# Raw first products of each later layer, corrected for the norm afterwards

## The chip, the cores and the metric

One core of one Trainium2 chip runs the whole program. The metric is the device time of one execution in microseconds (us). Engines are named as the profile does: PE (TensorE), DVE (VectorE), ACT (ScalarE), POOL (GpSimd), SP (the queue that issues the DMAs).

## What is computed

A model of three blocks over 512 positions of width 1024, all in float32: a first block (swiglu, a mixer, a second swiglu, then "ple", a gated product with a second input p, and a norm), and two layers of a second block. The parts around the change, cut from the reference:

```python
gate = jax.nn.sigmoid(rmsnorm(h, norm_ple[i]) @ w_ple_gate[i])
h = h + gate * (p[i] @ w_ple[i])
...
x = rmsnorm(h, norm_final)
for l in range(DEPTH_2):
    mod = c_act @ w_ada[l] + b_ada[l]
    shift, scale, gate = jnp.split(mod, 3, axis=-1)
    h = rms_norm(x, norm_g[l]) * (1.0 + scale[:, None, :]) + shift[:, None, :]
    u = h @ w_in[l]
    rg_x, rg_z, ml_x, ml_o, ml_z = jnp.split(u, split_pts, axis=-1)
    ...
    y = jnp.concatenate([y_rg, y_ml], axis=-1) @ w_out[l]
    x = x + gate[:, None, :] * y
```

A norm divides each position by the root of its mean square, so it is known only when all 1024 features of the position are there.

## The kernel before, in words

Activations lie with 128 features on the partitions and the 512 positions along a row; a width of 1024 is eight such tiles h(0) to h(7). A float32 product is made of three matmuls of 128x512 (`mm3`, L125 to L127): the input is split into a high and a low part (xnh by ACT, xnl by DVE), the weights into whi and wlo, and hi*hi, lo*hi and hi*lo are summed in PSUM. One such product of a 128x128 block takes three matmuls 0.227 us apart.

Weights come as one stream (`Stream`, L56): chunks of eight blocks, 512 KB, loaded by DMAs of the SP queue, split by ACT (whi, L96) and DVE (wlo, L98), two chunks ahead of their use. `hold` and `release` set these splits back at the end of ple and of out0.

A norm (`Norm`, L130) squares each tile as it is finished (ACT, L149), adds the squares on DVE (L155) and POOL (L153), lets PE sum the columns (L165), takes the root in ten small DVE steps (L206 to L213), spreads it over the partitions by four PE transposes (L195) and copies it to `nrow` (ACT, L198).

ple makes eight tiles h(m): the gate product, DVE multiplies it with nrow (L1282), ACT takes tanh (L1283), and two DVE steps (L1287, L1288) finish h. `between` (L1345 on) then makes two norms in one, and `modulate` makes the input of layer 0: per tile a multiply mt (DVE L1330 or POOL L1328), ACT xnh (L1337), DVE mx (L1338) and DVE xnl (L1341). Only then start the products. The first four of a layer (ml_x, outputs 16 to 19, here called raw products where they don't wait for the norm) give `cpad`, the input of a convolution on DVE (L1507, L1509), whose result, split as xch and xcl, feeds the next step, "qkv0". The order of the products behind is a written string `LAYER` (P24 and so on). At the end of each layer `out` makes the next x from 16 products a tile; in layer 0 `renorm` follows, which is the same chain once more (seam 1). While layer 0 runs, the normalised x is written to memory tile by tile and read back for the residual in out.

A list of small steps (`Fill`) that prepares the layers (the modulation from c, gates, constants) is run beside the swiglu of ffn2, with a rate R2; it also loads and splits p (pp0h, pp0l and so on).

Of the kernel before, what the change touches and what calls it, by code (L numbers as in the profile page):

```python
# [38 lines left out]
R1, R2 = 0.27, 0.26  # L39
# [8 lines left out]
GAPS = {"base": 288, "ffn1": 320, "ffn2": 0, "lay": 320, "mix2": 224, "ple": 256}  # L48
# [81 lines left out]
class Norm:  # L130
# [3 lines left out]
    def __init__(self, k, n, pool=None, tail=False):  # L134
        self.k, self.n, self.i = k, n, 0
        self.tail, self.head = tail, None
        self.pool = pool or k.work
        self.acc = []

    def add(self, src, scale=1.0):  # L140


        k, i = self.k, self.i
        own = i < 2 or (self.tail and i == self.n - 1)
        if own:
            sq = self.pool.tile([128, T], F32, name="nacc", bufs=3 if self.pool is k.work else 6)
# [3 lines left out]
        if own:  # L150
            self.acc.append(sq)
        elif i % 2:
            k.nc.gpsimd.tensor_add(self.acc[1], self.acc[1], sq)  # L153
        else:
            k.nc.vector.tensor_add(self.acc[0], self.acc[0], sq)  # L155
        self.i += 1
        if self.i == self.n - self.tail:
            eng = k.nc.vector if self.tail else k.nc.gpsimd
            eng.tensor_add(self.acc[0], self.acc[0], self.acc[1])
# [1016 lines left out]
def second_prepare(k, pool, ins):  # L1176
# [15 lines left out]
    for l in range(2):  # L1192
# [8 lines left out]
        L.bif = k.const2.tile([128, 8], F32, name=f"bif{l}")  # L1201
        L.v = lambda name, l=l: k.vec[:, VEC[f"{name}.{l}"][0]:VEC[f"{name}.{l}"][0] + VEC[f"{name}.{l}"][1]]
# [13 lines left out]
        def acc(i, L=L, boxes=boxes):  # L1216
# [3 lines left out]
                                   op0=OP.mult, op1=OP.add, accum_out=L.mod[:, i:i + 1])  # L1220

# [54 lines left out]
def ple(k, pool, xs, norm, pt, on_tile, early):  # L1276
# [3 lines left out]
    def gate1(m, pg):  # L1280
        ts[m] = pool.tile([128, T], F32, name="pleg", bufs=2)
# [16 lines left out]
    for m in range(8):  # L1298
# [12 lines left out]
        k.ws.hold = m == 7  # L1311
# [4 lines left out]
    early()  # L1316


def modulate(k, l, norm, gg, scr):
# [3 lines left out]
    xs, ts = [], []  # L1323
    with k.tc.tile_pool(name=f"modulate{l}", bufs=3) as tmp:
        def scale(d):
            t = tmp.tile([128, T], F32, name="mt", bufs=4)
# [4 lines left out]
            ts.append(t)  # L1331
        for d in range(3):
            scale(d)
        for d in range(8):
            x = tmp.tile([128, T], F32, name="mx")
            hi, lo = xtile(k, "xnh"), xtile(k, "xnl")
            nc.scalar.activation(hi, ts[d], AF.Identity, scale=gg[:, d:d + 1], bias=L.mod[:, d:d + 1])  # L1337
            v.tensor_scalar(x, ts[d], gg[:, d:d + 1], L.mod[:, d:d + 1], op0=OP.mult, op1=OP.add)  # L1338
            if d + 3 < 8:
                scale(d + 3)  # L1340
            v.tensor_sub(lo, x, hi.bitcast(F32))  # L1341
            xs.append((hi, lo))
            if d == 1:
                k.ws.release()
            k.dbg(f"hh{l}{d}", x)  # L1345
    return xs


def between(k, scr, nf, ng):
# [3 lines left out]
    nc, v = k.nc, k.nc.vector  # L1353
    gg = k.work.tile([128, 8], F32, name="gg")
    gf = k.vec[:, VEC["norm_final"][0]:VEC["norm_final"][0] + 8]
    v.tensor_mul(gg, gf, k.lay[0].gs)
    nf.part1(root=False)
    ng.mean()
    ms = k.work.tile([128, 4], F32, name="nmt", bufs=2)
    v.scalar_tensor_tensor(ms, nf.ms, 1e-6, ng.ms, op0=OP.mult, op1=OP.add)  # L1360
    ng.col = k.work.tile([128, 4], F32, name="ncol", bufs=2)
    rsqrt(k, ng.col, ms)
    ng.part2()
    xs = modulate(k, 0, ng, gg, scr)
    rsqrt(k, nf.col, nf.ms)

    def root():
        nf.part2()

    def residual(d):  # L1370
        v.scalar_tensor_tensor(k.h[d], k.h[d], gf[:, d:d + 1], nf.row, op0=OP.mult, op1=OP.mult)
        nc.sync.dma_start(scr["x"][d], k.h[d])
        k.dbg(f"x2{d}", k.h[d])
    return xs, [root] + [lambda d=d: residual(d) for d in range(8)]


def renorm(k, l, norm, scr):
    norm.part1()
    norm.part2()
    xs = modulate(k, l, norm, k.lay[l].gs, scr)  # L1380
    return xs, [lambda d=d: k.nc.sync.dma_start(scr["x"][d], k.h[d]) for d in range(8)]
# [85 lines left out]
def layer(k, l, xs, aside, ins, scr, norm, out):  # L1467
# [4 lines left out]
    with ExitStack() as st:  # L1472
        pool = st.enter_context(k.tc.tile_pool(name=f"lay{l}", bufs=1))
        room(pool, "lay")
# [750 lines left out]
```

## Time and profile before

| | |
|---|---|
| median of 3 runs | 1997.68 us (1996.73 to 1998.62) |
| profiled execution, its own time | 1996.86 us |
| its span in the trace | 1995.1 us |
| busy: PE, DVE, ACT, POOL | 1931.2, 1311.4, 821.4, 164.4 us |
| mean granted PE clock | 0.982 |

The span is what the trace covers; the rest of the time lies around it. Stages of the span: ffn2 690 to 1061, ple 1061 to 1119, seam 0 to 1137, layer 0 to 1555 (out0 from 1466), seam 1 to 1571, layer 1 with its ending to 1995. A busy share is an average: what a step is worth is read from the wait that it ends.

### The profile page before, as it was taken

The page shows a single profiled execution, that of the slowest core. Times are in us where ns is not written, and L with a number is a line of the kernel's source. Part 1 is how long each engine was busy: PE and PEld are TensorE (multiplying, and loading weights), DVE is VectorE, ACT ScalarE, POOL GpSimd, SP SyncE. Part 2 cuts the span into 40 slices and gives each one's busy share as a digit, 9 for nine tenths or more (in the row PEclk, how much of TensorE's full clock was granted, in tenths as well). Part 3 has the DMA queues.
Part 4 walks back from the last instruction along what each step waited for, and adds up shares of the span by engine and source line. Part 5 has one row for each costly group of instructions (what it writes and reads, how often), then busy time and mean ns, then how long its engine had stood idle before and what let it go on. Part 6 is the DMA issues. An engine that isn't in the chain of part 4 may idle for free. (4 is left out here: it accounts for less than half of the span.)

```text
span 1995.1 us, 24709 instructions
## 1 busy us (share of the span) xinstructions
PE 1931.2 (97%) x9320; PEld 1581.3 (79%) x9320; DVE 1311.4 (66%) x2157; ACT 821.4 (41%) x1233; POOL 164.4 (8%) x225
## 2 busy tenths in 40 slices
PE   8999999998999999999999799999999899999997
PEld 6888888887867888888878687888888677887886
DVE  7766576678655575665666675887763666877843
ACT  5323232436555432232244445555432354555521
POOL 1000000111233100000001100101000100101001
PEclk9999999998899999999999899999999899999999
DMA  5335445465301365455433143222242243222241
GB/s 184 103 116 154 158 139 159 143 194 171 103 1 33 117 218 180 158 197 190 162 104 92 55 147 118 74 75 86 88 153 87 64 156 109 70 89 86 74 155 56
DMA packets 101400, 240.10 MB, mean 120 GB/s; under 512 B 24472, under 2 KB 37528, under 8 KB 101280
## 3 DMA queue, kind: packets, MB, share of 16 engines
q1 hardware_dynamic: 100592, 237.82, 37.6%
q8 instruction: 73, 1.20, 0.2%
q10 hardware_dynamic: 688, 0.70, 0.1%
q14 instruction: 47, 0.39, 0.1%
HBM read 216.19 MB, written 21.10 MB: 119 GB/s over the span
## 5 line engine op out<-in xcount | busy, mean ns | idle before, releaser
L98 DVE TENSOR_TENSOR wlo<-wstage,whi 128x1024 fp32r<-128x1024 f32 (+1 forms) x305 | 377.3, 1245 | 147.6 <-ACT whi L96 143.8
L96 ACT ACTIVATE whi<-wstage 128x1024 fp32r<-128x1024 f32 (+1 forms) x306 | 314.0, 1045 | 139.9 <-PE pasecond L126 43.1
L276 ACT ACTIVATE t<-t 128x512 f32<-128x512 f32 x44 | 27.9, 634 | 158.5 <-DVE t L275 158.5
L127 PE MATMUL pahead<-xnh,wlo 128*128 128x512 f32 x208 | 81.3, 391 | 3.4 <-DVE wlo L98 3.4
L125 PE MATMUL pahead<-xnh,whi 128*128 128x512 f32 x208 | 83.3, 400 | 0.0
L153 POOL TENSOR_TENSOR nacc<-nacc,nsq 128x512 f32<-128x512 f32 x20 | 26.8, 1343 | 680.9 <-ACT nsq L149 680.9
L126 PE MATMUL pahead<-xnl,whi 128*128 128x512 f32 x208 | 81.1, 390 | 0.0
L125 PE MATMUL pbfirst<-xnh,whi 128*128 128x512 f32 x176 | 70.4, 400 | 7.6 <-ACT whi L96 6.5
L125 PE MATMUL pbhead<-xnh,whi 128*128 128x512 f32 x192 | 76.9, 400 | 0.0
L1509 DVE SCALAR_TENSOR_TENSOR conv<-cpad,vec,conv 128x512 f32<-128x512 f32 x96 | 72.2, 752 | 5.6
L127 PE MATMUL pbhead<-xnh,wlo 128*128 128x512 f32 x192 | 75.5, 393 | 0.0
L126 PE MATMUL pbhead<-xnl,whi 128*128 128x512 f32 x192 | 75.3, 392 | 0.0
L126 PE MATMUL pbfirst<-xnl,whi 128*128 128x512 f32 x176 | 69.5, 395 | 0.3 <-DVE xnl L222 0.3
L127 PE MATMUL pbfirst<-xnh,wlo 128*128 128x512 f32 x176 | 69.2, 393 | 0.0
L125 PE MATMUL pbsecond<-xnh,whi 128*128 128x512 f32 x176 | 68.9, 392 | 0.0
L125 PE MATMUL pafirst<-xnh,whi 128*128 128x512 f32 x176 | 68.7, 390 | 0.0
L127 PE MATMUL pafirst<-xnh,wlo 128*128 128x512 f32 x176 | 68.6, 390 | 0.0
L127 PE MATMUL pbsecond<-xnh,wlo 128*128 128x512 f32 x176 | 68.5, 389 | 0.0
L126 PE MATMUL pbsecond<-xnl,whi 128*128 128x512 f32 x176 | 68.5, 389 | 0.0
L126 PE MATMUL pafirst<-xnl,whi 128*128 128x512 f32 x176 | 68.5, 389 | 0.0
L127 PE MATMUL pasecond<-xnh,wlo 128*128 128x512 f32 x176 | 68.5, 389 | 0.0
L125 PE MATMUL pasecond<-xnh,whi 128*128 128x512 f32 x176 | 68.5, 389 | 0.0
(762 smaller groups left out, 5229.9 us busy)
## 6 DMA issues: line engine op xcount, KB each, us to landing
wstage<-in_wpack_dram SPq DMA_DIRECT2D x304, 512.0 KB, 3.7
adaw<-in_wada_dram SPq DMA_DIRECT2D x48, 512.0 KB, 4.5
scr_v<-vv SPq DMA_DIRECT2D x16, 256.0 KB, 2.2
vr<-scr_v SPq DMA_DIRECT2D x16, 256.0 KB, 4.4
xr<-scr_x SPq DMA_DIRECT2D x16, 256.0 KB, 5.8
h<-in_xT_dram SPq DMA_DIRECT2D x8, 256.0 KB, 5.8
s5vw<-scr_wq SPq DMA_DIRECT2D x64, 32.0 KB, 2.0
s5vb<-in_s5bq_dram SPq DMA_DIRECT2D x8, 256.0 KB, 2.7
```

Of the source, the lines that this page charges most:

```text
L96: k.nc.scalar.activation(hi[:, s], st[:, s], AF.Copy)
L98: eng.tensor_sub(lo[:, s], st[:, s], hi[:, s].bitcast(F32))
L125: mm(ps, w[0], x[0], start=start, stop=False)
L126: mm(ps, w[0], x[1], start=False, stop=False)
L127: mm(ps, w[1], x[0], start=False, stop=stop)
L153: k.nc.gpsimd.tensor_add(self.acc[1], self.acc[1], sq)
L276: nc.scalar.activation(t1, t1, AF.Silu)
L1509: v.scalar_tensor_tensor(c, xp[:, 1 + j:1 + j + T], w(j), c, op0=OP.mult, op1=OP.add)
```

## The change

- Raw products. Position by position, norm and shift can be applied after the product: (h g r + s) W = r (h g) W + s W. So h(m) times its gain is split as it is made (`split_raw`: ACT xnh, DVE xnl; in ple and in out0), and the four ml_x products run on it in the order RAW. `raw_pad` then multiplies with nrow (DVE) and adds s W (ACT). s W comes from new steps in the fill of ffn2: 16 transposes, 4 copies, 8 loads of 512 KB and 8 sums on DVE.
- Norm steps at other products. The sums, the root and the transposes hang as hooks at products 8, 10 and 14 of RAW in layer 0 and 1, 3 and 9 in layer 1; a tile of the proper input, for the products from P24 on, at every second product after. It takes two DVE steps and one of ACT; POOL has no part in it.
- p is loaded and split at the start of ple, in a pool that both layers share, and no longer in the fill.
- In ple h(m) is written to memory raw, and out0 makes the norm of the residual with four transposes and eight DVE steps.
- The adds of tile 6's squares in ple stand behind tile 7; hold and release are gone; R2 is 0.30, two gaps between pools are larger.

```diff
+def split_raw(k, src, g, hi, lo):
+    k.nc.scalar.activation(hi, src, AF.Copy, scale=g)
+    k.nc.vector.scalar_tensor_tensor(lo, src, g, hi.bitcast(F32), op0=OP.mult, op1=OP.subtract)
+    return hi, lo
...
 def modulate(k, l, norm, gg):
-            if d % 2:
-                nc.gpsimd.tensor_mul(t, k.h[d], norm.row)
-            else:
-                v.tensor_mul(t, k.h[d], norm.wide)
...
-            nc.scalar.activation(hi, ts[d], AF.Identity, scale=gg[:, d:d + 1], bias=L.mod[:, d:d + 1])
-            v.tensor_scalar(x, ts[d], gg[:, d:d + 1], L.mod[:, d:d + 1], op0=OP.mult, op1=OP.add)
-            v.tensor_sub(lo, x, hi.bitcast(F32))
...
+        v.scalar_tensor_tensor(t, k.h[d], g, norm.wide if d == 0 else norm.row, op0=OP.mult, op1=OP.mult)
+        nc.scalar.activation(hi, t, AF.Identity, bias=b)
+        v.scalar_tensor_tensor(lo, t, b, hi.bitcast(F32), op0=OP.add, op1=OP.subtract)
...
+RAW = [(m, d) for m in range(4) for d in range(7)]
+RAW = RAW[:14] + [(0, 7)] + RAW[14:21] + [(1, 7)] + RAW[21:] + [(2, 7), (3, 7)]
+def seam(k, l, norm, gg, early, mean, at):
+    xs, tile = modulate(k, l, norm, gg)
+    hooks = dict(zip(at, (early, mean, norm.part2)))
+    for d in range(8):
+        hooks[at[2] + 1 + 2 * d] = lambda d=d: tile(d)
+    return xs, hooks
...
 def layer(k, l, raw, xs, hooks, aside, before, ins, scr, norm, out):
+        def raw_pad(i, ps):
...
+            v.tensor_mul(xp[:, 4:], ps, before.row)
+            nc.scalar.activation(xp[:, 4:], xp[:, 4:], AF.Identity, bias=L.sw[:, i:i + 1])
...
-        for m, ps in enumerate(proj4([16, 17, 18, 19])):
-            ml_pad(m, ps)
+        for n, (i, d) in enumerate(RAW):
+            mm3(k, banks[i], k.ws.get((win, d, 16 + i)), raw[d], d == 0, d == 7)
+            if n in hooks:
+                hooks[n]()
+            if d == 7:
+                raw_pad(i, banks[i])
...
+                nc.tensor.transpose(pb[:, j * 128:(j + 1) * 128], k.closing[:, j:j + 1].to_broadcast([128, 128]), k.ident)
+            if l == 0:
+                v.scalar_tensor_tensor(xr[m], xr[m], k.v("norm_final", m), pb, op0=OP.mult, op1=OP.mult)
...
+            if l == 0:
+                raw.append(split_raw(k, k.h[m], k.lay[1].gs[:, m:m + 1], xtile(k, "xnh"), tile("xnl", F32R)))
+                nc.sync.dma_start(scr["x"][1, m], k.h[m])
...
+        def done(m):
+            if m == 6:
+                raw.append(split_raw(k, k.h[m], gg[:, m:m + 1], k.ytile("xnh", F32R), k.ytile("xnl", F32R)))
+            nf.add(k.h[m], 1.0, later if m == 6 else None)
+            ng.add(k.h[m], k.v("norm_final", m), later if m == 6 else None)
+            for f in later if m == 7 else ():
+                f()
+            if m != 6:
+                raw.append(split_raw(k, k.h[m], gg[:, m:m + 1], k.ytile("xnh", F32R), k.ytile("xnl", F32R)))
+            nc.sync.dma_start(scr["x"][0, m], k.h[m])
...
+        for i in (1, 2, 3):
+            step(1.4, sacc, i)
```

The first place is ACT at the end of ffn2: gh is the split of a swiglu tile, t its gate, p the second input of ple. Before:

```order
431 L233 ACTIVATE gh<-t_8344 128x512
432 L96 ACTIVATE whi<-wstage 128x1024 x2
433 L233 ACTIVATE pp0h<-p_8415 128x512
434 L233 ACTIVATE pp1h<-p_8417 128x512
435 L276 ACTIVATE t_8427<-t_8427 128x512
436 L233 ACTIVATE gh<-t_8428 128x512
437 L221 ACTIVATE xnh<-h,vec 128x512
```

Now:

```order
438 L96 ACTIVATE whi<-wstage 128x1024
439 L283 ACT_TABLE_LOAD
440 L283 ACTIVATE t_8473<-t_8473 128x512
441 L240 ACTIVATE gh<-t_8474 128x512
442 L228 ACTIVATE xnh<-h,vec 128x512
```

The copies pp0h and pp1h are gone from here; they stand 20 rows on, at the start of ple, and a table load has come up to the last tile.

The second place is DVE in ple, one tile after another (h is its result, pleg its gate). Before:

```order
1087 L1282 TENSOR_TENSOR pleg<-pbple,nrow 128x512
1088 L98 TENSOR_TENSOR wlo<-wstage,whi 128x1024
1089 L1287 SCALAR_TENSOR_TENSOR pleg<-pleg,paple 128x512
1090 L1288 SCALAR_TENSOR_TENSOR h<-pleg,h 128x512
1091 L1282 TENSOR_TENSOR pleg<-pbple,nrow 128x512
```

Now:

```order
1117 L1319 TENSOR_TENSOR pleg<-pbple,nrow 128x512
1118 L98 TENSOR_TENSOR wlo<-wstage,whi 128x1024
1119 L1324 SCALAR_TENSOR_TENSOR pleg<-pleg,paple 128x512
1120 L1325 SCALAR_TENSOR_TENSOR h<-pleg,h 128x512
1121 L1357 SCALAR_TENSOR_TENSOR xnl<-h,gg,xnh 128x512
1122 L1319 TENSOR_TENSOR pleg<-pbple,nrow 128x512
```

The raw xnl, which needs ACT's xnh of the same tile, stands between h and the gate multiply of the next tile.

The third place is DVE behind the root of the norm in seam 0. Before:

```order
1115 L213 SCALAR_TENSOR_TENSOR ncol<-rsa,rsy 128x4
1116 L1330 TENSOR_TENSOR mt<-h,pm 128x512 x2
1117 L1338 TENSOR_SCALAR mx<-mt,gg,mod_5923 128x512
1118 L1341 TENSOR_TENSOR xnl<-mx,xnh 128x512
1119 L1338 TENSOR_SCALAR mx<-mt,gg,mod_5923 128x512
1120 L1330 TENSOR_TENSOR mt<-h,pm 128x512
1121 L1341 TENSOR_TENSOR xnl<-mx,xnh 128x512
```

Now:

```order
1150 L98 TENSOR_TENSOR wlo<-wstage,whi 128x1024
1151 L1529 TENSOR_TENSOR cpad<-pagates_9195,nrow 128x512
1152 L1370 SCALAR_TENSOR_TENSOR mt<-h,gg,pm 128x512
1153 L1373 SCALAR_TENSOR_TENSOR xnl<-mt,mod_5924,xnh 128x512
1154 L1370 SCALAR_TENSOR_TENSOR mt<-h,gg,nrow 128x512
1155 L1373 SCALAR_TENSOR_TENSOR xnl<-mt,mod_5924,xnh 128x512
```

Each xnl now follows its own mt directly, with ACT's xnh between them, and the multiplies that make cpad lie among the tiles.

## Rows read from the trace of the kernel before

**Rows 1.** The page, busy time of each engine (us, share of the span, instructions).

```profile
PE 1931.2 (97%) x9320; PEld 1581.3 (79%) x9320; DVE 1311.4 (66%) x2157; ACT 821.4 (41%) x1233; POOL 164.4 (8%) x225
```

**Rows 2.** Timeline of PE, ple, seam 0, qkv0 (start, duration, what; wait and releaser in brackets).

```profile
1061.33 0.39 PE L125 MATMUL paple<-xnh,whi 128*128 128x512 f32 x1
...
1118.17 0.39 PE L127 MATMUL pbple<-pp1h,wlo 128*128 128x512 f32 x1
...
1131.10 0.66 PE L195 MATMUL pm<-ident,ncol 128*128 128x128 f32 x2 [2.52 <-DVE ncol L213]
...
1134.45 0.79 PE L125 MATMUL pagates<-xnh,whi 128*128 128x512 f32 x1 [2.26 <-ACT xnh L1337]
...
1179.00 0.39 PE L126 MATMUL pbgates<-xcl,whi 128*128 128x512 f32 x1
```

**Rows 3.** Timeline of PE, end of out0 and qkv0 of layer 1.

```profile
1554.36 0.39 PE L127 MATMUL pbout<-ymh,wlo 128*128 128x512 f32 x1
...
1606.97 0.39 PE L126 MATMUL pbgates<-xcl,whi 128*128 128x512 f32 x1
```

**Rows 4.** Windows, seam 0 (span; busy PE, PEld, DVE, ACT, POOL; clock, DMA share, GB/s).

```profile
1124.00:1140.00 16.00, 8.91 (x29) 7.27 (x30) 9.67 (x26) 7.37 (x10) 3.79 (x3) 0.50 0.00 0
```

**Rows 5.** Timeline of PE, last tile of ffn2.

```profile
1036.21 0.49 PE L125 MATMUL pasecond<-gh,whi 128*128 128x512 f32 x1 [2.33 <-ACT gh L233]
```

**Rows 6.** Timeline of ACT, the split of p near the end of ffn2.

```profile
1030.18 0.63 ACT L233 ACTIVATE pp0h<-p 128x512 fp32r<-128x512 f32 x1 [4.53 <-DMA p<-in_pT_dram]
```

**Rows 7.** One line of PE, transposes (minimum/median/maximum ns, first and last start).

```profile
L1022 PE MATMUL pc<-ident,csm x8: 272/272/273, 555.3 to 556.0; 128*128 128x128 f32 x8
```

**Rows 8.** One line of DVE, the sums of the modulation in ffn2, same columns.

```profile
L1219 DVE CUSTOM_DVE_ANT_0 adaj<-adaw,b2c,vec x48: 1274/1278/1282, 710.2 to 1013.7; 128x1024 f32<-128x1024 f32 x48
```

**Rows 9.** Timeline of DVE, end of ffn2 and ple.

```profile
1053.06 0.68 DVE L305 SCALAR_TENSOR_TENSOR h<-pasecond,h 128x512 f32<-128x512 f32 x1
1054.53 0.75 DVE L222 SCALAR_TENSOR_TENSOR xnl<-h,vec,xnh 128x512 fp32r<-128x512 f32 x1 [0.80 <-ACT xnh L221]
1055.20 0.69 DVE L155 TENSOR_TENSOR nacc<-nacc,nsq 128x512 f32<-128x512 f32 x1
...
1075.97 1.23 DVE L98 TENSOR_TENSOR wlo<-wstage,whi 128x1024 fp32r<-128x1024 f32 x1 [1.65 <-ACT whi L96]
1077.12 0.68 DVE L1287 SCALAR_TENSOR_TENSOR pleg<-pleg,paple 128x512 f32<-128x512 f32 x1
1077.83 0.69 DVE L1288 SCALAR_TENSOR_TENSOR h<-pleg,h 128x512 f32<-128x512 f32 x1
...
1114.96 1.65 DVE L98 TENSOR_TENSOR wlo<-wstage,whi 128x1024 fp32r<-128x1024 f32 x1 [2.25 <-ACT whi L96]
...
1123.61 0.69 DVE L1288 SCALAR_TENSOR_TENSOR h<-pleg,h 128x512 f32<-128x512 f32 x1
```

**Rows 10.** Timeline of ACT, a tile of ple, and nrow of seam 0.

```profile
1112.20 0.63 ACT L149 ACTIVATE nsq<-h 128x512 f32<-128x512 f32 x1 [2.67 <-DVE h L1288]
1112.74 0.71 ACT L149 ACTIVATE nsq<-h,vec 128x512 f32<-128x512 f32 x1
1113.36 0.61 ACT L1283 ACTIVATE pleg<-pleg 128x512 f32<-128x512 f32 x1
1113.88 1.05 ACT L96 ACTIVATE whi<-wstage 128x1024 fp32r<-128x1024 f32 x1
...
1132.23 0.60 ACT L198 ACTIVATE nrow<-pm 128x512 f32<-128x512 f32 x1 [6.65 <-PE pm L195]
```

**Rows 11.** Timeline of DVE, first convolution of layer 0 and its second xcl.

```profile
1159.85 0.55 DVE L1507 TENSOR_SCALAR conv<-cpad,vec 128x512 f32<-128x512 f32 x1 [1.99 <-ACT cpad L1501]
...
1177.52 0.68 DVE L1546 TENSOR_TENSOR xcl<-xcs,xch 128x512 fp32r<-128x512 f32 x1
```

**Rows 12.** Timeline of POOL, adds of squares in ple.

```profile
1112.98 2.55 POOL L153 TENSOR_TENSOR nacc<-nacc,nsq 128x512 f32<-128x512 f32 x2 [13.62 <-ACT nsq L149]
```

More of the change, by code (lines that the diff above doesn't have):

```diff
@@ L130, with __init__, add @@
 class Norm:
[L134 removed]
+    def __init__(self, k, n, new=None, tail=False):
         self.k, self.n, self.i = k, n, 0
         self.tail, self.head = tail, None
[L137 removed]
+        self.new = new or (lambda name: k.work.tile([128, T], F32, name=name, bufs=3))
         self.acc = []
[L140 removed]
+    def add(self, src, scale=1.0, later=None):
         k, i = self.k, self.i
@@ L145, in add @@
         if own:
-            sq = self.pool.tile([128, T], F32, name="nacc", bufs=3 if self.pool is k.work else 6)
+            sq = self.new("nacc")
         else:
@@ L1349, in between @@
[L1349 to L1374, printed above, removed]
@@ L1377, in renorm, with tile @@
[L1377 to L1381, printed above, removed]
+    xs = []
+    def tile(d):
+        t = k.ytile("mt")
+        g, b = gg[:, d:d + 1], L.mod[:, d:d + 1]
+        v.scalar_tensor_tensor(t, k.h[d], g, norm.wide if d == 0 else norm.row, op0=OP.mult, op1=OP.mult)
+        hi, lo = xtile(k, "xnh"), xtile(k, "xnl")
+        nc.scalar.activation(hi, t, AF.Identity, bias=b)
+        v.scalar_tensor_tensor(lo, t, b, hi.bitcast(F32), op0=OP.add, op1=OP.subtract)
+        xs.append((hi, lo))
@@ new lines, in modulate, with between, early, mean @@
+    return xs, tile
+RAW = [(m, d) for m in range(4) for d in range(7)]
[6 more added lines that the diff above has]
+    return xs, hooks
+def between(k, nf, ng, gg):
+    v = k.nc.vector
+    def early():
+        nf.early()
+        ng.early(0.0)
+    def mean():
+        nf.mean()
+        ng.mean()
+        ms = k.work.tile([128, 4], F32, name="nmt", bufs=2)
+        v.scalar_tensor_tensor(ms, nf.ms, 1e-6, ng.ms, op0=OP.mult, op1=OP.add)
+        ng.col = k.work.tile([128, 4], F32, name="ncol", bufs=2)
+        rsqrt(k, ng.col, ms)
+    return (*seam(k, 0, ng, gg, early, mean, (8, 10, 14)), [lambda: rsqrt(k, k.closing, nf.ms)])
@@ L1464, in ending, with layer @@
     last(1, 6, False, nc.sync)
-def layer(k, l, xs, aside, ins, scr, norm, out):
+def layer(k, l, raw, xs, hooks, aside, before, ins, scr, norm, out):
     nc, v = k.nc, k.nc.vector
@@ L2088, in body @@
-        norm = None
+            swiglu(k, st["xs"], st["norm"], "ffn2_w1", "ffn2_w3", "ffn2_w2", (6, 6, 5, 5),
+                   lambda d: feed("norm_ple", d), R2, ((0, 1, 5), (1, 0, 7)), "ffn2")
+            k.fill.drain()
+        k.phase = "ple"
+        k.lpool = pool("lay")
+        room(k.lpool, "lay")
+        k.ytile = lambda name, dtype=F32: k.lpool.tile([128, T], dtype, name=name, tag="y", bufs=k.NX)
+        pt = []
+        for d in range(2):
+            t = k.ytile(f"p{d}")
+            nc.sync.dma_start(t, ins["pT"][d * 128:(d + 1) * 128])
+            pt.append(t)
@@ new lines, in body @@
+        for d in range(2):
+            hi, lo = k.ytile(f"pp{d}h", F32R), k.ytile(f"pp{d}l", F32R)
+            nc.scalar.activation(hi, pt[d], AF.Copy)
+            nc.vector.tensor_sub(lo, pt[d], hi.bitcast(F32))
+            pt[d] = hi, lo
+        nf, ng = Norm(k, 8, k.ytile, True), Norm(k, 8, k.ytile, True)
+        gg = k.work.tile([128, 8], F32, name="gg")
+        gf = k.vec[:, VEC["norm_final"][0]:VEC["norm_final"][0] + 8]
+        nc.vector.tensor_mul(gg, gf, k.lay[0].gs)
+        raw = []
@@ L2089, in body @@
+        ple(k, st["xs"], st["norm"], pt, done)
+        before = ng
+        xs, hooks, aside = between(k, nf, ng, gg)
         for l in range(2):
@@ L2091, in body @@
             k.phase = f"layer{l}"
-            layer(k, l, xs, aside, ins, scr, norm, out)
+            raw = layer(k, l, raw, xs, hooks, aside, before, ins, scr, norm, out)
             if l == 0:
-                xs, aside = renorm(k, 1, norm, scr)
+                before = norm
+                xs, hooks, aside = renorm(k, 1, norm)
         return k.ws
```

139 lines of the change are left out of this document (65 added, 74 removed).

## The prediction

> **What bounds the kernel now.** I read the page first: TensorE is busy for 97% of the span, VectorE for 66% [rows 1]. A change can therefore win only where TensorE stands, and the waits by stage say where. Two places concern this change: the seam between ple and layer 0, and the one between the product "out" of layer 0 and layer 1. In the timeline of the first, the last ple product starts at 1118.17 and ends 0.39 later, at 1118.56. The first product of the layer starts at 1134.45, and ahead of it, at 1131.10, stand the four transposes of the norm [rows 2]; each of these steps has waited for another engine. The second seam has the same chain behind 1554.75, where out0 ends [rows 3]. The seam costs clock as well: from 1124 to 1140 the granted clock is 0.50, TensorE's lower level of 1.2 GHz, while little runs on it [rows 4].
>
> The landmark I use is the second product matmul of qkv0, which needs the split xcl: from there on the program and its waits are alike in both kernels. It starts at 1179.00 in layer 0, 117.67 after ple's first product (1061.33), and at 1606.97 in layer 1, 52.2 after the end of out0 [rows 2, 3]. I sum the change against these two numbers.
>
> **ffn2: about -0.7.** The last swiglu tile of ffn2 makes TensorE wait 2.33 [rows 5]. ScalarE is why: the copy pp0h stood 4.53 for the DMA of p, and the tile's own steps stand behind it [rows 6]. The change takes pp0h out of this queue, so I take 2.33 off; what can be late next is the table load that now stands there, which at most gives these 2.33 back. Against it come 16 transposes of the shifts. Eight of the same form start between 555.3 and 556.0 [rows 7], 0.1 each: +1.6. The eight sums on VectorE (1.28 each by the rows of their like [rows 8], 10.2 in all) lie in a phase in which it has idle time; with that cover gone they would cost up to 10.
>
> **ple: the pace passes to VectorE and ScalarE.** Two p splits of VectorE, 0.69 each like its adds [rows 9], now stand ahead of the norm's root: h of tile 0, which ended at 1078.52 [rows 9], comes 1.3 later. If p lands late it is up to 3 more. Then each tile's chain grows. Today tile 0 to tile 7 end from 1078.52 to 1124.30 [rows 9], 6.54 a tile, while TensorE takes 6.8 (ten products of three matmuls, 0.227 apart). Tanh of the next tile lies right behind the squares today [rows 10]. By the order shown with the change, the raw split now lies between. Along the new chain: squares 0.54 and 0.62 [rows 10], xnh 0.80 with its hand-overs (VectorE's idle time ahead of an xnl of the same form) and xnl 0.67 [rows 9], the gate multiply as long as the last step, 0.69, tanh 0.52 and whi 1.08 up to the start of wlo [rows 9, 10], wlo 1.15, and the two last steps 0.71 and 0.69 [rows 9]: 7.5. Seven tiles are 52.5 instead of 45.8, +6.7. (One tile has a second wlo, +1.2; in tile 6 the split goes ahead of the squares, -1.2.) So h of tile 7 comes at 62.97+1.3+6.7=71.0 after ple's start. TensorE's slack of two banks hides part of this, so ple itself may lengthen by 3 or so, but the chain goes on from h and not from TensorE.
>
> **Seam 0 and qkv0: +5.1 in all.** Four VectorE adds that used to lie ahead of the last tile now follow it: 4x0.65=2.6. From the last h to the end of nrow it takes 1132.83-1124.30=8.5 [rows 9, 10]; I keep that, as the sums, the ten root steps and the transposes are the same: nrow at 82.1. Nine raw products, 6.1, run meanwhile; TensorE then waits some 4 to 5 for the sums. Next come eight tiles, each a VectorE step, a ScalarE step and a VectorE step in strict order. The same trio in ffn2, h, xnh, xnl, runs from 1053.06 to 1055.20 [rows 9], 2.14 a tile, 17.1 in all. With them stand four multiplies that make the conv input (0.6 each) and two wlo (1.4 with the wait for whi): 22.3. Convolution starts at 104.4, today at 1159.85-1061.33=98.5. From its start to the end of the xcl that qkv0 wants, today is 1178.21-1159.85=18.4 [rows 11]; nothing in that piece changes. The landmark comes at 122.8 instead of 117.7: **+5.1**. The raw products take TensorE's wait away, and it waits at the tiles, at wlo and at xcl instead, because VectorE is the slower one from ple to qkv0.
>
> **out0: +0.4** for four transposes that normalise the residual. Eight raw splits and eight residual steps lie in tiles of 48 matmuls, 10.9, where VectorE has two wlo and little else: nothing; with that cover gone 0.75 each.
>
> **Seam 1 and qkv0: -1.4.** Here no tile of VectorE work is behind: nine raw products (6.1) cover the root, and from the transposes to the end of nrow it takes 1.7, as in seam 0 [rows 2, 10]. With a wlo in front I put nrow at 8.5. The tiles take 17.1, four multiplies 2.4, three wlo 4.2, then 18.4: 50.8 instead of 52.2. If the wlo's are hidden it is -5; if nrow comes as late as in layer 0, +2.
>
> **GpSimd.** Its multiplies of the seam go; I give that no price of its own, since the trio's 2.14 is taken where GpSimd is idle. In ple its adds of squares stay, two pairs of 2.55 [rows 12], and the new xnl lies beside them. The nearest row says that little happens: the last wlo of ple, 1.65 beside a pair, is 0.42 over the 1.23 alone [rows 9].
> The Trainium skill's page "SBUF — State Buffer", section "🔬 SBUF: two separate sides", says more: a VectorE operation with two SBUF inputs and a GpSimd one that reads SBUF exclude each other for the whole instruction. By that my estimate is a landmark later by two whole adds, and a sum of +6. The trace agrees only in part: the row of 1.65 shows a stretch of a third of an add.
>
> **Sum.** -0.7+5.1+0.4-1.4=+3.4 on the profiled execution's 1996.86, which stands 0.8 below the median of the runs shown: **2001.1** for the median. A measurement tells about 0.2%, 4 us, from no change, so this is at the edge of it.
>
> **Rivals.**
> *F, faster: the chain is shorter than I sum it.* Place: the ple tile and the tiles of the proper input. The sum of single rows counts every hand-over in full. If the ple tile stays at TensorE's 6.8 (5 less) and a tile of the proper input takes 1.6 (VectorE busy without its 0.80 wait; 4 to 5 less in either layer), the sum is 3.4-14=-11: about 1987. At the far end TensorE alone decides: to either landmark it needs 56 products of 0.68, 38, beside the sums, so some 10 in either layer would be left to win and ple would not lengthen: about 1973. It decides from the point where the xcl is ready before its product. For it speaks that both seams lose clock and time openly; against it, that VectorE's queue is in order.
> *M, layer 1 pays.* Layer 0 goes as above, but in layer 1 the wlo's lie in the waits for xnh: -5 there, 1997 in all.
> *S, slower: the weight loads come late.* In ple eight writes of h now stand in the SP queue between loads of weights, each waiting for its h. A chunk lasts TensorE 5.4 (eight products of 0.68), so the look-ahead of two chunks is 10.9. Without a row for it I bound the price by the tiles: an h that comes up to 8 late holds the load behind it, and from the point where load, whi and wlo no longer fit into 10.9 TensorE waits, at most the 1 by which the new tile exceeds the old, seven times: +7 on the sum, 2008. Against it: the write needs only h, which is there before the splits.
> *P, slower: GpSimd shuts out xnl.* Where a pair of adds has begun, xnl of that tile waits for one whole add, 1.3 (half of the 2.55), twice in ple; h is late by 2.6 and with it the landmark: 2003.7. The stretched wlo speaks for it, its small size against. The Trainium skill's rule above is this case.
>
> **How the numbers follow.** The forecast (1997 to 2005, with a late p at its upper end) gets 0.40, F 0.28, M 0.12, S 0.14, P 0.06. Faster: F but for its upper end, and a third of M, 0.30. Slower: S, P and half of the forecast, 0.40. The rest, 0.30, is within 0.2%. The range runs from 1984, which takes in the middle of F, to 2010, S and a late p together; F's far end stays out.
>
> **What would show it.** Right: no wait of 2.3 at ffn2's last tile; h of tile 7 some 8 us later after ple's start; raw products right behind ple; nrow in layer 0 near 82 after ple's start; waits at xnh, wlo and xcl adding up to 10 or more ahead of qkv0; landmarks at 122.8 and 50.8. Wrong: a ple tile near 6.8, or landmarks at 112 and 46 and less, would mean F; waits for whi whose load landed just before would mean S.

## The result and the profile after

The changed kernel takes 2008.66 us (median of five; 2006.76 to 2010.60) against 1997.68 (median of five; 1996.73 to 2001.39): **1.0051 times the kernel before, 95% interval 1.0037 to 1.0066**. It is slower, as forecast, and inside the range, but by 11.0 where the sum said 3.4, and outside the 1997 to 2005 of the forecast itself. Its profiled execution, 2006.76 with a span of 2005.0, is the fastest of its five; against the span before it is 9.9 longer. The stages of the two traces, in us:

| stage | before | after | difference | predicted |
|---|---|---|---|---|
| start, and ffn2 to ple's first product | | | -2.9 | -0.7 |
| ple's first product to the product that reads the second xcl | 118.36 | 126.40 | +8.0 | +5.1 |
| from there to out0's first product | 286.90 | 289.17 | +2.3 | 0 |
| out0 | 88.16 | 87.33 | -0.8 | +0.4 |
| end of out0 to the product that reads the second xcl | 52.92 | 52.30 | -0.6 | -1.4 |
| from there to the heads of layer 1 | 95.40 | 98.13 | +2.7 | 0 |
| heads of layer 1 to out1 | 190.50 | 191.72 | +1.2 | 0 |
| sum | | | +9.9 | +3.4 |

The mark here is the first product that reads the second xcl, one step behind the mark of the prediction, which was the first product that reads the first one; why is told below.

Timeline of PE of the changed kernel, to be laid beside [rows 2, 3]:

```profile
1058.46 0.39 PE L125 MATMUL paple<-xnh,whi 128*128 128x512 f32 x1
...
1131.50 3.54 PE L172 MATMUL pm<-ones,nacc 128*128 128x1 f32 x16 [4.01 <-DVE nacc L162]
1137.61 2.19 PE L172 MATMUL pm<-ones,nacc 128*128 128x1 f32 x16
1142.47 0.60 PE L202 MATMUL pm<-ident,ncol 128*128 128x128 f32 x4
...
1175.47 0.50 PE L127 MATMUL pagates<-xnh,wlo 128*128 128x512 f32 x1 [1.03 <-DVE wlo L98]
1184.86 0.50 PE L126 MATMUL pbgates<-xcl,whi 128*128 128x512 f32 x1 [3.63 <-DVE xcl L1581]
...
1604.27 0.50 PE L127 MATMUL pagates<-xnh,wlo 128*128 128x512 f32 x1 [3.33 <-DVE wlo L98]
1613.66 0.79 PE L126 MATMUL pbgates<-xcl,whi 128*128 128x512 f32 x1 [3.62 <-DVE xcl L1581]
```

Raw products do run right behind ple. PE then waits for the sums' operand, for a wlo and for xcl; the transposes stand at 1142.47, 84.0 after ple's first product, where they stood at 69.8 before.

The DVE and ACT rows that answer to [rows 9, 10, 11]: the last ple tile, the copy nrow, the first tiles of the proper input, the convolution and the second xcl.

```profile
1129.26 0.69 DVE L1325 SCALAR_TENSOR_TENSOR h<-pleg,h 128x512 f32<-128x512 f32 x1
...
1144.35 0.74 DVE L1370 SCALAR_TENSOR_TENSOR mt<-h,gg,pm 128x512 f32<-128x512 f32 x1
1145.88 0.75 DVE L1373 SCALAR_TENSOR_TENSOR xnl<-mt,mod,xnh 128x512 fp32r<-128x512 f32 x1 [0.79 <-ACT xnh L1372]
1146.55 0.74 DVE L1370 SCALAR_TENSOR_TENSOR mt<-h,gg,nrow 128x512 f32<-128x512 f32 x1
...
1166.62 0.54 DVE L1543 TENSOR_SCALAR conv<-cpad,vec 128x512 f32<-128x512 f32 x1
...
1184.12 0.68 DVE L1581 TENSOR_TENSOR xcl<-xcs,xch 128x512 fp32r<-128x512 f32 x1
```

```profile
1143.11 0.60 ACT L205 ACTIVATE nrow<-pm 128x512 f32<-128x512 f32 x1 [9.37 <-PE pm L202]
```

h(7) ends at 1129.95, 71.5 after ple's first product; nrow at 85.2; the convolution starts at 108.2, the second xcl ends at 126.3. A tile of the proper input takes 2.20, and in each of them DVE stands 0.79 for ACT.

Windows of the changed kernel around the sums (span; busy PE, PEld, which is PE's weight loads, DVE, ACT, POOL with instructions; clock, DMA share, GB/s), and over the time behind the second xcl of layer 1 and one place in the heads:

```profile
1132.00:1138.00 6.00, 6.00 (x24) 5.42 (x23) 2.72 (x5) 1.74 (x2) 0.00 (x0) 0.50 0.51 164
1138.00:1144.00 6.00, 6.00 (x36) 5.29 (x36) 3.52 (x15) 0.60 (x1) 0.00 (x0) 0.97 0.00 0
...
1612.00:1620.00 8.00, 6.34 (x16) 5.00 (x17) 5.86 (x8) 4.33 (x8) 0.10 (x1) 0.57 0.29 86
1725.00:1730.00 5.00, 5.00 (x16) 3.93 (x16) 3.36 (x5) 2.61 (x4) 0.00 (x0) 0.66 0.14 20
```

This is the new thing. The kernel before also shows 0.50 in its seam [rows 4], but there PE had little to run. Here, from 1132 to 1138, PE is busy all the time at its lower level of 1.2 GHz. The first sums take 3.54, and the second ones stand behind two raw products that take 2.71 from start to start (1134.90 to 1137.61), where two take 1.36 at 0.227 a matmul. The root and the transposes follow the second sums.

### The profile page after: what moved, and what is told of

Read it like the earlier page. It is cut to its first block, busy times and chain, and to the rows that moved or that the text cites. A ratio compares the mean times of both kernels' runs of the same rounds, so it can differ in the third digit from the quotient of the medians.

```text
span 2005.0 us, 24794 instructions
## 1 busy us (share of the span) xinstructions
PE 1937.3 (97%) x9336; PEld 1581.3 (79%) x9336; DVE 1330.1 (66%) x2189; ACT 830.5 (41%) x1252; POOL 157.4 (8%) x217
```

## The experiments

Two theories. **Chain**: the path h(7), squares, sums, root, transposes, nrow, tiles, convolution sets the time, and what PE does beside it costs nothing. **Clock**: the path runs through PE's queue twice (sums, transposes), so a fall of the clock lengthens it. The letters in the expectations change: "theory A" is the chain in e2_pipe, e3_defer and e5_busy, and the clock in e7_late_sums and e11_sums_15. Ratios are to the kernel before on the same chip. "Two stages" means ple's first product to the product that reads the second xcl (126.40 in the changed kernel). Here and below nrow and h(7) are ends after ple's first product.

### e2_pipe: the tile of the proper input, pipelined

```diff
         nc.scalar.activation(hi, t, AF.Identity, bias=b)
-        v.scalar_tensor_tensor(lo, t, b, hi.bitcast(F32), op0=OP.add, op1=OP.subtract)
+        return lambda: v.scalar_tensor_tensor(lo, t, b, hi.bitcast(F32), op0=OP.add, op1=OP.subtract)
...
+    def piped(d):
+        if d < 8:
+            open_.append(tile(d))
+        if d:
+            open_.pop(0)()
```

> The changed kernel, with one thing moved: VectorE does the first step of the next input tile before the last step of this one, so that it doesn't stand 0.8 us a tile for ScalarE. Theory A (VectorE's chain from the last h to xcl sets when qkv0 goes on): nrow to the first convolution takes about 17 us instead of 22.9, the waited xcl matmul of qkv0 comes 5 to 6 us earlier in either layer, and the whole is 9 to 12 us faster than the changed kernel, ratio to before 0.9985 to 1.001. Rival B (the loss is the half clock after single long waits, and TensorE's own work sets the rest): less than 3 us, ratio 1.0035 to 1.0055.

Measured: 1998.29, ratio 1.0011 (0.9999 to 1.0022), just outside theory A's range and far from B's. Timeline of its DVE:

```profile
1146.70 0.75 DVE L1370 SCALAR_TENSOR_TENSOR mt<-h,gg,nrow 128x512 f32<-128x512 f32 x1
1147.58 0.75 DVE L1374 SCALAR_TENSOR_TENSOR xnl<-mt,mod,xnh 128x512 fp32r<-128x512 f32 x1
1148.24 0.75 DVE L1370 SCALAR_TENSOR_TENSOR mt<-h,gg,nrow 128x512 f32<-128x512 f32 x1
```

A tile now takes 1.3 to 1.6 instead of 2.20, the 0.79 is gone, and from nrow to the convolution it is 17.9 instead of 22.9. In layer 1 the stage falls from 52.30 to 47.26, all of it. In layer 0 the two stages fall by 2.2 only, 124.16: nrow came at 88.05 there instead of 85.2. The tiles are on the path in both layers.

The late nrow is a first price of the clock. Up to the transposes PE, DVE and ACT run the same instructions in the same order as in the changed kernel, and the first sums start 73.06 after ple's first product, there 73.04. But the transposes come at 86.8, there at 84.0; the clock stays low for longer (the changed kernel's window from 1138 to 1144 has 0.97):

```profile
1144.17 0.60 PE L202 MATMUL pm<-ident,ncol 128*128 128x128 f32 x4
```

```profile
1138.00:1144.00 6.00, 6.00 (x22) 5.15 (x22) 3.26 (x14) 0.00 (x0) 0.00 (x0) 0.57 0.00 0
```

### e3_defer: the raw split behind the next tile's tanh

```diff
+            pending.append(lambda: raw.append(split_raw(k, k.h[m], gg[:, m:m + 1], k.ytile("xnh", F32R), k.ytile("xnl", F32R))))
...
         if m:
             gate1(m, pgs[m])
+        while pending:
+            pending.pop(0)()
```

> The changed kernel, with the raw split of a ple tile issued behind the tanh of the next tile instead of ahead of it. Theory A: the ple tile falls from 7.5 to 6.8 us or less, h of tile 7 comes some 6 us earlier after ple's start (65 instead of 71.5), ple itself is 3 to 4 us shorter, and all of the 6 us arrives at the xcl matmul of layer 0; layer 1 is as it was. Ratio to before 1.0015 to 1.0025. Rival S (late weight loads behind the writes of h) or P (GpSimd's adds shut xnl out): the tile stays above 7.2 us and the ratio at 1.004 to 1.006.

Measured: 2007.2, ratio 1.0052 (1.0036 to 1.0069), a miss. h(7) comes at 66.95, 4.5 earlier (6 expected), yet nrow only 1.0 earlier, at 84.2. PE and one window of it:

```profile
1127.01 1.02 PE L172 MATMUL pm<-ones,nacc 128*128 128x1 f32 x8 [2.12 <-DVE nacc L162]
...
1132.81 3.41 PE L172 MATMUL pm<-ones,nacc 128*128 128x1 f32 x16
1141.35 0.74 PE L202 MATMUL pm<-ident,ncol 128*128 128x128 f32 x4
```

```profile
1132.00:1138.00 6.00, 6.00 (x24) 5.42 (x23) 1.63 (x10) 0.00 (x0) 0.00 (x0) 0.50 0.14 57
```

The sums are early, the transposes are not: the last root step on DVE ended at 1138.59, and the transposes stood in PE's queue for 2.8 more. The chain theory, by which the products beside the chain cost nothing, can't explain that; the clock is 0.50 from 1132 to 1138.

### e5_busy: products that keep PE busy in the waits

```diff
+                if l == 0 and n == 8:
+                    idle(raw[0][0], 17)
...
+                        if h + ki + mo == 1 and ki and name == "ml_w_q":
+                            idle(xm[0][0], 15)
```

> The changed kernel with idle work for TensorE: 17 matmuls of 128x512 whose result nobody reads ahead of the first sums in layer 0, where it waits 4.0 us, and 15 ahead of the xcl matmul that waits 3.6 us, in both layers. Rival B (the half clock costs): the granted clock stays at 1.00 behind these three places, and 4 to 6 us are won, ratio 1.002 to 1.003. Theory A alone (VectorE's chain sets the time, clock or not): the clock stays up and at most 2 us are won, as what stands behind is VectorE's, ratio 1.004 to 1.0055.

Measured: 2005.77 (1999.78 to 2012.79), ratio 1.0049 (1.0033 to 1.0065). Inconclusive: the runs lie 13 apart. At the sums PE waited 0.38 only, but the clock fell all the same, for a shorter time (0.50 from 1134 to 1136, 0.72 from 1132 to 1138), and nrow came 1.1 earlier, at 84.18. Behind the second xcl of layer 0 the clock stood at 1.00, and the stretch to the heads took 96.51, in the changed kernel 97.15, before 95.19. In layer 1 the added products came after another wait and made PE 2.3 late, and the stretch behind was 2.9 shorter: one against the other.

### e6_p_early: p loaded earlier in the kernel before

```diff
-                k.fill.steps += [(0.1, load_p), (0.1, lambda: None), (1.2, split_p)]
+                k.fill.steps[4:4] = [(0.1, load_p)]
+                k.fill.steps += [(1.2, split_p)]
```

> The kernel before, with p loaded early in ffn2 and split where it was. If the DMA of p was what held the last swiglu tile back, its wait of 2.33 us goes and nothing takes its place: 2.0 to 2.6 us faster than before, ratio 0.9987 to 0.999. Rival: the tile waits for something else then, ratio 1.000.

Measured: 1995.59, ratio 0.9997 (0.9985 to 1.0008): too small to be told by the time. By stage it can: ffn2 is 2.8 shorter, and the waits of its PE for gh and gl fall from 3.8 to 1.3. The waits of PE in ffn2 (us in total, times, longest), before:

```profile
PE pasecond L125 <- ACT gh L233: 3.1, 2, 2.3
PE pasecond L126 <- DVE gl L234: 0.7, 3, 0.2
```

In the changed kernel all but 0.2 of these 3.8 is gone. ffn2 is 2.4 shorter (373.67 to 371.26), so 1.2 is left for the 16 transposes and the rest of the new fill.

### e7_late_sums: the sums at later products, in the changed kernel

A tile follows at each product instead of each second, and the products of the last raw tile of the first two outputs move back with them (22 and 25).

```diff
-    return (*seam(k, 0, ng, gg, early, mean, (8, 10, 14)), [lambda: rsqrt(k, k.closing, nf.ms)])
+    return (*seam(k, 0, ng, gg, early, mean, (16, 17, 21)), [lambda: rsqrt(k, k.closing, nf.ms)])
```

> The changed kernel with only one thing moved: in seam 0 the two sums, the transposes and the modulate tiles hang behind later raw products (16th, 17th and 21st on, a tile at each product instead of each second), so that TensorE has products left to run until the sums' operand is there. The chain h(7) -> square -> sums -> n2 -> products -> transposes -> nrow -> tiles is the same instruction for instruction. Theory A (half clock): the changed kernel's 4.01 us wait at the first sums drops the granted clock to 0.50 for about 6 us, and the chain's own short products then stand in TensorE's queue behind raw products at half speed, which is the +3.1 us by which nrow came later than predicted. Then here: wait at the first sums under 1.5, clock 1.00 over the 12 us around them, nrow's end at 82 to 83 us after the input projection's start (85.2 in the changed kernel), the stage from the projection's end to the first awaited split operand 60 to 61.5 (63.7), total ratio to the kernel before 1.003 to 1.0045. Rival B (the chain alone sets the time, TensorE's clock beside it costs nothing): nrow at 85 again, stage 63.5 to 64, ratio 1.005 as the changed kernel.

Measured: 2006.93, ratio 1.0050 (1.0038 to 1.0062). A miss for the clock theory as I had put it: no wait at the sums any more, but nrow at 85.75 (h(7) was 0.9 later there too) and the two stages 127.55. Its PE:

```profile
1136.66 2.07 PE L172 MATMUL pm<-ones,nacc 128*128 128x1 f32 x16
1142.88 0.60 PE L202 MATMUL pm<-ident,ncol 128*128 128x128 f32 x4
```

```profile
1138.00:1144.00 6.00, 6.00 (x25) 4.94 (x25) 1.96 (x12) 0.49 (x1) 0.00 (x0) 0.72 0.28 99
```

From sums to transposes it takes 6.2, part of it at the lower level (0.57 from 1138 to 1140), although PE's last wait, 0.44, had ended at 1120.2. So it is not the wait at the sums alone that brings the clock down. Part of the late nrow is the places themselves: the first sums started at 1133.88, 1.8 behind their operand, and the transposes 1.8 behind the last root step.

### e8_pipe_defer and e9_all: both edits, then with later sums

The first is the two edits of e2_pipe and e3_defer together.

> The two edits e2_pipe (the next tile's multiply and activation go ahead of this tile's residue) and e3_defer (the raw split of an input projection tile goes behind the next tile's tanh) together. If both gains lie on the path one after the other: the projection stage 58.2 (62.7 in the changed kernel), the stage behind it 61.5 + 3.5 - 4.9 or so = 62 to 64, layer 1's seam 47.3 (52.3), sum about 1.0 to 2 us below e2_pipe: ratio 0.9995 to 1.0010. The half-clock theory says the deferral gives 1 us, not 4.5, because the 2 us wait at the sums still drops the clock. The theory without the clock says 6 us below e2_pipe: ratio 0.997 to 0.9985.

Measured: 1994.34, ratio 0.9982 (0.9972 to 0.9992), which is the range of the theory without the clock. But both executions paid for the clock alike: from h(7) to nrow it takes 17.0 here (nrow at 83.92) and 16.5 in e2_pipe, so the 4.6 of the deferral come out nearly whole. To this the places of the sums were added, with a tile at each product (last raw tile at 19 and 24):

```diff
-    return (*seam(k, 0, ng, gg, early, mean, (8, 10, 14)), [lambda: rsqrt(k, k.closing, nf.ms)])
+    return (*seam(k, 0, ng, gg, early, mean, (13, 14, 18)), [lambda: rsqrt(k, k.closing, nf.ms)])
```

> e8_pipe_defer with the sums, transposes and tiles of seam 0 hung behind later raw products as in e7_late_sums (13th, 14th and 18th on), so that no product waits at the sums. Half-clock theory: with no wait at the sums the 4.5 us of the deferral arrive in full: the sum of the projection stage and the one behind it is 2.5 to 4 us shorter than in e8_pipe_defer, and the ratio 0.9965 to 0.9985 (below the kernel before). Rival (chain alone): within 1 us of e8_pipe_defer.

Measured: **1988.47, ratio 0.9956 (0.9944 to 0.9968)**, faster than the kernel before. nrow at 77.93, 6.0 earlier, the two stages 113.15 instead of 120.05, more than either theory had. Places and clock changed together here. PE of the first, then of the second, each with a window:

```profile
1126.67 3.24 PE L172 MATMUL pm<-ones,nacc 128*128 128x1 f32 x16 [2.15 <-DVE nacc L162]
1132.47 3.41 PE L172 MATMUL pm<-ones,nacc 128*128 128x1 f32 x16
1140.86 0.60 PE L202 MATMUL pm<-ident,ncol 128*128 128x128 f32 x4
```

```profile
1132.00:1138.00 6.00, 6.00 (x23) 5.39 (x22) 1.90 (x12) 0.00 (x0) 0.00 (x0) 0.50 0.08 32
```

```profile
1127.85 1.84 PE L172 MATMUL pm<-ones,nacc 128*128 128x1 f32 x16
1130.35 1.84 PE L172 MATMUL pm<-ones,nacc 128*128 128x1 f32 x16
1134.90 0.60 PE L202 MATMUL pm<-ident,ncol 128*128 128x128 f32 x4
```

```profile
1132.00:1138.00 6.00, 6.00 (x30) 4.96 (x30) 3.78 (x15) 1.65 (x3) 0.00 (x0) 1.00 0.34 126
```

The sums run 1.2 later and the transposes 6.0 earlier. With the clock at 1.00 it is 11.0 from h(7) to nrow; the prediction had 11.1.

### e10_all_busy: that version with PE kept busy in the wait for xcl

It is the version above with 15 unread products ahead of the product that waits for the second xcl, in both layers.

> e9_all with 15 products into a bank that nobody reads (512 columns each) ahead of the gate product that waits 3.6 us for the split convolution tile, in both layers: TensorE is kept busy for the length of that wait and nothing else changes; the products' result is not used. If the half clock after that wait costs what e5_busy's layer 1 hinted (98.1 -> 95.2 for the stretch behind it), each layer gets 2 to 3 us back: 4 to 6 us below e9_all, ratio 0.994 to 0.9965. If the wait itself is the whole price: the same as e9_all, or up to 1 us slower by the products' overshoot.

Measured: 1988.46, ratio 0.9959 (0.9944 to 0.9974): no difference. In layer 1 the clock is held, and the wait is filled; windows of layer 1, without the products and with them:

```profile
1592.00:1598.00 6.00, 3.53 (x9) 2.80 (x10) 5.65 (x9) 3.56 (x6) 0.10 (x1) 0.74 0.22 65
```

```profile
1592.00:1598.00 6.00, 5.80 (x25) 4.20 (x24) 5.87 (x9) 3.01 (x5) 0.10 (x1) 1.00 0.15 32
```

The stretch behind falls from 96.97 to 96.52 only. The 2 to 3 that I expected there are not to be had: in this version the clock was low for a short time only.

### e11_sums_15 and e12_defer_sums: the sums less late, alone and with the deferral

```diff
-    return (*seam(k, 0, ng, gg, early, mean, (8, 10, 14)), [lambda: rsqrt(k, k.closing, nf.ms)])
+    return (*seam(k, 0, ng, gg, early, mean, (14, 15, 19)), [lambda: rsqrt(k, k.closing, nf.ms)])
```

> e7_late_sums moved the sums too far: its second sum, products and transposes came behind four products that stood there at a granted clock of 0.57, and nrow came no earlier. Here the changed kernel again with only the places moved, and less: sums behind the 14th and 15th raw product, transposes behind the 19th, a tile at each product behind that. Second sum's operand at about 75.6 us after the projection's start by e7_late_sums, sums to transposes 4.6 by e9_all, so transposes at 80 to 81 and nrow's end at 81 to 82 (85.2 in the changed kernel) if the clock stays at 1.00. Theory A (half clock in TensorE's queue): nrow 3 to 4 earlier, the two stages from the projection's start to the split operand 122.5 to 124 (126.4), ratio 1.0030 to 1.0045. Theory C (the waits for the last tile set nrow and the clock falls all the same, as in e7_late_sums without any wait at the sums): nrow at 84 to 86, 126 to 127.5, ratio 1.0045 to 1.0055.

Measured: 2008.20, ratio 1.0056 (1.0042 to 1.0069); nrow at 86.43, the clock at 0.50 from 1136 to 1142. A miss for theory A, and at or just above the upper ends of theory C.

The second is the deferral of above with the places (13, 14, 18).

> e3_defer (raw split of a projection tile behind the next tile's tanh, nothing pipelined) with the sums and transposes of seam 0 behind the 13th, 14th and 18th raw product, as in e9_all. e3_defer alone gave h(7) 4.5 us earlier, and kept 1.0 of it at nrow (84.2 after the projection's start). From e8_pipe_defer to e9_all the same move took nrow from 83.9 to 77.9. If the half clock behind the wait at the sums is what ate the 4.5: nrow at 77.5 to 78.5, the two stages 119 to 120.5 (125.4 in e3_defer), ratio 1.0020 to 1.0030 against 1.0052. If it was the pipelined tiles of e9_all that gave the gain: as e3_defer, ratio 1.0045 or more.

Measured: 2002.02, ratio 1.0016 (1.0003 to 1.0030), below both ranges, while the profiled execution has nrow at 81.07 and the two stages at 122.2, between the two cases. Its 11 runs lie from 1995.14 to 2006.94, three times as wide as those of the changed kernel, and the profiled one is the slowest. So it was run once more.

### e13_again and e14_after_again: the same programs once more

> The program of e12_defer_sums once more, to see another execution of it. Its profiled execution was the slowest of 11 (2006.94; the fastest 1995.14), and in it the granted clock fell to 0.50 at 1132 to 1138, ahead of the transposes, although TensorE had not waited at the sums. If such falls differ between executions of one program, a faster one shows no 0.50 between sums and transposes, nrow at 77.5 to 78.5 after the projection's start as in e9_all (81.1 in the slow one), and each missing fall makes it 3 to 4 shorter: 1996 to 2002. If the program fixes them, the same stretch stands at 0.50 again, nrow at 81 and the time is 2005 to 2008.

Measured: 2001.28. PE of the first execution of this program, with a window, and of the second:

```profile
1128.76 1.84 PE L172 MATMUL pm<-ones,nacc 128*128 128x1 f32 x16
1131.26 2.82 PE L172 MATMUL pm<-ones,nacc 128*128 128x1 f32 x16
1138.98 0.60 PE L202 MATMUL pm<-ident,ncol 128*128 128x128 f32 x4
```

```profile
1132.00:1138.00 6.00, 6.00 (x20) 5.13 (x21) 2.11 (x13) 0.00 (x0) 0.00 (x0) 0.50 0.48 165
```

```profile
1128.31 1.84 PE L172 MATMUL pm<-ones,nacc 128*128 128x1 f32 x16
1130.81 1.84 PE L172 MATMUL pm<-ones,nacc 128*128 128x1 f32 x16
1135.36 0.60 PE L202 MATMUL pm<-ident,ncol 128*128 128x128 f32 x4
```

```profile
1132.00:1138.00 6.00, 6.00 (x32) 5.04 (x32) 2.71 (x13) 1.20 (x2) 0.00 (x0) 1.00 0.42 158
```

One program, two executions: h(7) is at 66.91 in both and the first sums start at 69.6 in both; from there the clock is the difference that the rows show. nrow comes at 81.07 and at 77.87, and the two stages are 122.2 and 119.0. **The price of the half clock in this chain is 3.2**, and it comes out in full at the second xcl. With e2_pipe's 2.8 in the changed kernel's own order, that settles chain against clock.

> The changed kernel once more, unchanged. Its five runs lie within 4 us, against 12 in e12_defer_sums. If the 4.0 us wait at its sums brings the clock down each time: 0.50 between sums and transposes again, nrow at 85 after the projection's start, 2006 to 2011. If the fall there is chance as well: nrow near 82 and 2003 to 2006.

Measured: 2008.28. The fall at the sums is there again (0.52 from 1132 to 1138), nrow at 85.2, the two stages 126.34. Two windows of this execution show the clock elsewhere:

```profile
1612.00:1620.00 8.00, 6.02 (x27) 4.52 (x28) 6.46 (x9) 5.88 (x10) 0.10 (x1) 1.00 0.32 97
1830.00:1840.00 10.00, 10.00 (x36) 8.07 (x36) 7.53 (x26) 1.79 (x3) 0.00 (x0) 0.66 0.43 148
```

Behind the second xcl of layer 1 the clock did not fall this time, and that stretch is 96.52 instead of 98.13. It fell ahead of it instead (0.72 from 1604 to 1610), where PE went on to wait for xcl all the same. In the heads it fell twice, and they are 195.15 instead of 191.72.

## Why the prediction was right in sign and too small

**What held.** The ple tile: predicted 7.5, measured 7.47 to 7.54 in five of seven; h(7) at 71.0, measured 71.5. Two misses in that cancel in part: h(0) came 0.7 later and not 1.3, and the tile with the second wlo took 9.77 and not 8.7. From nrow to the convolution 22.3, measured 22.9; from there to the second xcl 18.4, measured 18.2. That VectorE and ScalarE set the pace, and that PE's waits go to the sums, xnh, wlo and xcl, is as the text had it, though those at xnh, xnl, wlo and xcl add up to 7.0 and not to 10; the sums have 4.0 beside them.

**A step that failed: "From the last h to the end of nrow it takes 8.5; I keep that, as the sums, the ten root steps and the transposes are the same".** By that step, with the adds that follow, h(7) to nrow is 11.1. It is 13.8. The work behind h(7) is not the same. PE before, while DVE finished the last ple tile and behind it:

```profile
1120.33 1.02 PE L165 MATMUL pm<-ones,nacc 128*128 128x1 f32 x8 [1.78 <-DVE nacc L159]
1121.73 1.02 PE L165 MATMUL pm<-ones,nacc 128*128 128x1 f32 x8 [0.38 <-DVE nacc L159]
1125.02 3.57 PE L165 MATMUL pm<-ones,nacc 128*128 128x1 f32 x16 [2.26 <-ACT nacc L149]
```

Half of the sums ran there before h(7) ended, at 1124.30. In the changed kernel all 32 follow h(7), 16 at 1131.50 and 16 at 1137.61, and raw products lie between them, so the norm pays for every product ahead of its sums, and nearly twice when the clock is at 0.50. The prediction read the 0.50 in [rows 4], called it a cost of the seam, and gave it no price in the new one. An estimate of that price from rows: the sums take 3.54 and 2.19 where 1.84 is their time at 1.00 (e13_again), the two products between them 2.71 instead of 1.36, together 3.4. In the three executions where the clock stood at 1.00 through the chain (e9_all, e10_all_busy, e13_again, with the sums at later products) h(7) to nrow is 11.0. That this is the 11.1 of the prediction is luck: its 8.5 held 16 sums at 0.50, the 11.0 holds 32 at 1.00. The step is 2.7 of the 6.5 that the sum lacks; h(7) adds 0.5.

**The larger step that failed: "from there on the program and its waits are alike in both kernels".** The sum had 0 behind the second xcl. It is 6.2. In layer 0 it is +2.3, of which 0.3 are out0's transposes (see there) and 2.0 lie ahead of the heads; e5_busy, which holds the clock there at 1.00, leaves 1.3 of these, so 0.6 is clock. In layer 1 it is +2.7; by the two executions of the changed kernel 1.6 is clock, and 1.1 is left with the clock at 1.00. Of what is left, 0.6 in either layer is a wait of PE for ScalarE's ml_w_q, seen in e5_busy (at 1188.10) and in e14_after_again (at 1617.69); the rest of it, 0.5 to 0.7, stays open. In layer 1's heads it is +1.2, and the row with 0.66 lies in that.

**A landmark set wrong.** The prediction took 117.7 (PE at its first xcl, where PE itself was the late one) and set against it 122.8, the time of the second xcl. In the kernel before the second xcl ended at 116.9 and PE came for it at 118.4. Like against like, the working gives +4.4 and not +5.1; measured +8.0. In layer 1 the same slip hides that the old xcl was ready 1.2 ahead of PE; there the terms add up to 50.6, not 50.8, and like against like they give -2.3 and not -1.4. Both slips lean towards slower, and so towards what was measured, by luck.

**ffn2, -0.7.** The term took the one wait of 2.33 off. The view of all waits there has 3.8, of which 0.2 is left; 1.2 by the rest goes to the transposes, for which the term had 1.6, and what else the fill does. So -2.4 and a start 0.5 earlier.

**out0, +0.4** measured -0.8. The four transposes take 0.35 (1473.68 to 1474.03), but ahead of out0's first product, so they stand in the row above it. The -0.8 are eight sums of the norm that stood in out0's last tile before (1549.56 to 1550.36) and now stand behind out0.

**Seam 1, -1.4** measured -0.6. nrow came at 9.7 instead of 8.5: the last root step ended at 1567.97, and the transposes, hung behind the ninth product, ran only at 1569.83, with the clock at 1.00. From nrow to the convolution it takes 24.3 where the terms have 23.7.

**The range.** That 2008.66 lies in it is luck in part. Its upper end was there for S and a late p, and neither came. The measured time is S's 2008 with another cause.

**The rivals.** F is out as the change stands: the ple tile is not 6.8 and the tile of the proper input not 1.6. Reordered, that tile is 1.3 to 1.6, and with the deferral and later sums the time is 1988.5, close to F's 1987: F's price was right for a kernel that takes the hand-overs away, not for this one. M needed hidden wlo's among the tiles of layer 1; there nrow to the convolution takes 24.3, and without three wlo it would be 19.5 by the terms. S needed waits for late weight loads; none of PE's matmuls in ple and the seams waits for whi, and no whi there waits for a DMA. P needed xnl shut out by GpSimd. Two rows of DVE and one of POOL, in ple of the changed kernel:

```profile
1100.75 0.75 DVE L1357 SCALAR_TENSOR_TENSOR xnl<-h,gg,xnh 128x512 fp32r<-128x512 f32 x1 [1.99 <-ACT xnh L1356]
1101.70 2.03 DVE L98 TENSOR_TENSOR wlo<-wstage,whi 128x1024 fp32r<-128x1024 f32 x1 [0.20 <-ACT whi L96]
```

```profile
1099.57 3.08 POOL L157 TENSOR_TENSOR nacc<-nacc,nsq 128x512 f32<-128x512 f32 x2 [33.91 <-ACT nsq L149]
```

xnl takes 0.75, as it does alone, so it is not shut out, and P is out. What is stretched lies around it: the second add of the pair takes 1.84 (1100.82 to 1102.66) and the first 1.29, and the wlo behind takes 2.03 against 1.23. The rule of the Trainium skill's page "SBUF — State Buffer", section "🔬 SBUF: two separate sides", is that a VectorE operation with two SBUF inputs and a GpSimd one that reads SBUF exclude each other for the whole instruction: the one that starts first runs, and the other waits. These rows fit it within 0.2, with xnl ahead of the second add and the wlo behind it; as POOL's spans are rough, they neither prove nor refute it.

## What to carry to other kernels

When a norm's sums and transposes are laid between other products, each product ahead of them is part of the norm's chain, and its price has to be taken at the clock that the rows show there, with the half clock as the upper bound. Ask also which steps stood ahead of the last tile and now follow it. A chain of DVE, ACT, DVE per tile leaves DVE standing for ACT, 0.79 a tile here; issue the next tile's first step ahead of this tile's last one. Hang a step at the product that runs when its operand is ready: too early it makes PE wait (4.0 at the sums of the changed kernel), too late it stands behind products that nothing needs yet (the transposes of seam 1, 1.9 behind the root).

## What the hardware showed that I had not expected

The granted clock fell to 0.50 in stretches in which PE had not stood just before: 1132 to 1138 in one execution of the deferral with later sums, with no wait at the sums and PE busy throughout (its last waits, 1.14 and 0.29, had ended by 1123.4; what it ran just before were the one-column sums, from 1128.76 and from 1131.26). Another execution of the same program, with the same waits, kept 1.00 there. The two took 2006.94 and 2001.28, with 3.2 of the difference in this one place; they ran on two chips, but on the first of these alone the 11 runs span 1995.14 to 2006.94. In the changed kernel the fall behind the 4.0 us wait at the sums was there in both executions seen, and again in e2_pipe; the one behind the second xcl of layer 1 was there in one of the two only, and those in the heads came at other places (1725 to 1730 in one, 1830 to 1840 in the other). With the sums moved so that PE had little or nothing to wait for (at most 1.16, in e11_sums_15), the fall came in e7_late_sums, in e11_sums_15 and in one execution of e12_defer_sums, and not in e9_all, e10_all_busy or the other execution. What decides it stays open.
